# A two-layer hybrid decoder on one Trainium2 core: decay matrices made where they are used, first tiles in another order, a norm factor applied one step later

## The chip, the core and the metric

The kernel runs on one core of a Trainium2 chip. Four engines work side by side, each in the order of its own instruction list: TensorE (PE: matrix products and transposes into PSUM; its weight loads are shown apart as PEld), VectorE (DVE), ScalarE (ACT) and GpSimd (POOL). SyncE (SP) issues nearly all DMAs, also in order: a DMA that has to wait for its data holds up those behind it. The metric is the device time of one execution in microseconds; the time before is the median of three runs.

## The reference

Two layers (DEPTH = 2) of a parallel-branch block on x of 512 x 1024, float32:

```python
h = rmsnorm(x, pre_mix_g)
proj = h @ w_in                     # split: DeltaNet q,k,v,z,beta,decay | SWA q,k,v | gates A,B
y_a = deltanet_branch(...) @ w_up_dn
y_b = swa_sink_branch(...) @ w_up_sw
mix = (sigmoid(gate_a) * y_a + sigmoid(gate_b) * y_b) @ w_o
x = x + rmsnorm(mix, post_mix_g)
ff = square(relu(rmsnorm(x, pre_mlp_g) @ w_ff1)) @ w_ff2
x = x + rmsnorm(ff, post_mlp_g)

# in the DeltaNet branch, per head and chunk, after a causal conv and silu on q, k, v:
g = cumsum(g)
decay = where(i >= j, exp(g_i - g_j), 0)
L = strictly_lower((k * beta) @ k.T * decay);  u, w = solve(I + L, ...)
a_intra = q @ k.T * decay
# scan over the chunks:  v_new = u - w S;  o = q exp(g) S + a_intra v_new;  S = exp(g_last) S + k_dec.T v_new
o = rmsnorm(o, norm_g) * silu(z)
```

DeltaNet has 8 heads of width 128; the sliding-window attention (SWA) has 16 query and 2 key heads of width 64, window 128, with a sink per head.

## The kernel before

All large products are made in three passes on values split in two (`_h` and `_l`): each weight block `wr` (128 x 1024, 512 KB) is loaded by SP, cast to `wh` on ScalarE and its remainder `wl` taken on VectorE (`prefetch`, lines 419 and 420). `weights()` hands out one split block and has the splits made LOOK = 4 blocks ahead; six `wr` buffers stand before them. One unit (`mm_a`, lines 435 to 437) is 24 matmuls of 512 columns into one of two PSUM buffers (`PM`). The kernel is written as one Python program; a planner puts each engine's instructions in order by their place in the program, by when their inputs are ready in its own model of times, and by free buffers. Only where the code opens an `Order` is the written order kept.

A layer runs in stages:

- the first products of a layer (`ps_b`: beta, decay, SWA k and v) for the four token tiles. In layer 0 their order on TensorE, ScalarE, VectorE and SP is written out by hand, with x loaded, normalized (`half`, tile `xs`), transposed (`turn`, `turned`) and the first three weight blocks split (`feed(0)` to `feed(2)`) in between.
- eight SWA query units (`ps_qf`). `q_out` scales and splits each and writes it to the scratch memory `qd`. At the third of them, `decays()` makes the running decay sums, writes them to `gd` (32 x 128), and then, for all eight heads in a loop, the 128 x 512 matrix D: a broadcast load from `gd`, a triangular select on GpSimd, `egl` (the decay of a whole chunk) and four exponentials on ScalarE, and a write to the scratch memory `dd`.
- 16 steps, each with one unit (k of a DeltaNet head, or a gate) and one attention group (`att_group`), whose queries `qT` come from `qd`. A k unit has two halves: `k_unit(h)` up to its `yield` makes the product, conv and silu and stores k; the rest, which is run one step later, loads D from `dd` (line 891), multiplies k by k (`ps_a`) and scales it with D (line 912) into `uu` for the triangular solve. D and `uu` share the four buffers of the tag `T[5]`.
- `solve()`, the up-projection of the attention (`ps_us`), and the DeltaNet heads in turn: `d_chain(h)` is the scan over four chunks (`ps_ks`, `rr` at line 1329, `ps_y` at line 1332, `ps_su`, `St`), beside it `d_dense(h+1)` makes v, q and z of the next head. D is loaded a second time from `dd` there (line 1231).
- the norm of a head's output is a generator, `d_tail(h)`: the mean square goes out to `sd`, comes back as `ff`, gets its power on GpSimd, goes out to `fd`, comes back broadcast as `fb`, and line 1288 multiplies `y1` (`yf`) with it. `d_step` runs the next piece of the heads it names, so each piece lies one call of `d_step` after the one before.
- the up-projection, output projection and the feed-forward part, which the diff does not touch.

Of the kernel before, what the change touches and what calls it, by code (L numbers as in the profile page):

```python
# [10 lines left out]
F32 = mybir.dt.float32  # L11
F32R = mybir.dt.float32r
# [8 lines left out]
P = 128  # L21
# [4 lines left out]
H = 8  # L26
# [117 lines left out]
def hybrid_trunk(ctx, tc, x, positions, pre_mix_g, dn_conv_w, dn_a_log, dn_dt_bias, dn_norm_g,  # L144
# [449 lines left out]
    def turned(ps, t, q):  # L594
        hi, lo = [c4(q[i])[:, :, t * P:(t + 1) * P] for i in range(2)]
        nc.scalar.copy(hi, c4(ps))
        tt(out=lo, in0=c4(ps), in1=hi.bitcast(F32), op=ALU.subtract)
# [52 lines left out]
    for l in range(depth):  # L650
# [4 lines left out]
        if l == 0:  # L655
            order = Order(nc.tensor, nc.scalar, nc.vector, nc.sync)
            order.begin()
            xts = [X4("x0") for t in range(NT)]
            gb, qs, hT = pre_begin(0)
            for i in range(2):  # L660
                dma(xts[0][:, i * 512:(i + 1) * 512], x[0:P, i * 512:(i + 1) * 512])
            wrs = []
            for t in (None, 1, None, 2, None, 3):
                if t is None:
                    wrs.append(load(specs[len(wrs)][0]))
                else:
                    dma(xts[t], x[t * P:(t + 1) * P, :])
            sq = lambda t: (meansq(xts[t][:, :512], "nq0"), meansq(xts[t][:, 512:], "nq1"))
            part = lambda t, a, b: mm_bkv(pb0[t][:, nbs], pre, hT, t, range(a, b))
            half = lambda t, g: norm_half(xts[t], gb, rs[t], g)  # L670
            feed = lambda j: prefetch(j + 1, wrs[j])

            def spin(n):

                for _ in range(n):
                    tr(pb0[2][:, 0:P], ident, ident)

            rs = [root(xts[0])]
            spin(5)
            xs = [half(0, 0), half(0, 1)]  # L680
            ps0 = [turn(x_) for x_ in xs]
            spin(5)
            feed(0)
            turned(ps0[0], 0, qs[0])
            q = [meansq(xts[1][:, :512], "nq0")]
            feed(1)
            q.append(meansq(xts[1][:, 512:], "nq1"))
            rs.append(rstd("nr", *q))
            part(0, 0, 2)
            turned(ps0[1], 0, qs[1])  # L690
            part(0, 2, 4)
            feed(2)
            q = sq(2)
            xs = [half(1, g) for g in range(2)]
            part(0, 4, 5)
            ps1 = [turn(x_) for x_ in xs]
            rs.append(rstd("nr", *q))
            part(0, 5, KT)
            for g in range(2):
                turned(ps1[g], 1, qs[g])  # L700
            q = sq(3)
            xs = [half(2, g) for g in range(2)]
            part(1, 0, 5)
            ps2 = [turn(x_) for x_ in xs]
            rs.append(rstd("nr", *q))
            part(1, 5, KT)
            for g in range(2):
                turned(ps2[g], 2, qs[g])
            xs = [half(3, g) for g in range(2)]
            part(2, 0, 5)  # L710
            ps3 = [turn(x_) for x_ in xs]
            part(2, 5, KT)
            for g in range(2):
                turned(ps3[g], 3, qs[g])
            pb0.append(PS("ps_b"))
            part(3, 0, KT)
            rotary()
            order.end()
            used[0] = 3
        else:  # L720
            hT = hT[2]
            ws = [weights() for _ in BK]
            part = lambda t, a, b: mm_bkv(pb0[t][:, nbs], ws, hT, t, range(a, b))
            part(0, 0, 5)
            part(1, 0, 5)
            part(0, 5, KT)
            part(1, 5, KT)
            qf0 = PZ("ps_qf")
            wq0 = weights()
            mm_a2(qf0, hT, 0, wq0, range(0, 4))  # L730
            norm_turn(xs_next[2], 2, nxt[1])
            mm_a2(qf0, hT, 0, wq0, range(4, KT))
            norm_turn(xs_next[3], 3, nxt[1])
            for a, b in ((0, 5), (5, KT)):
                for t in (2, 3):
                    part(t, a, b)
            mm_a2(qf0, hT, 1, wq0)
            order.end()
# [59 lines left out]
        def decays():  # L798
            ps = PS("ps_g")
            mm(ps[:, 0:32], lhsT=le, rhs=lw, start=True, stop=True)  # L800
            nc.vector.tensor_copy(gc, ps[:, 0:32])
            ts(out=ngc, in0=gc, scalar1=-1.0, scalar2=None, op0=ALU.mult)
            act(out=neg, in_=gc, func=AF.Exp)
            ts(out=neg, in0=neg, scalar1=-1.0, scalar2=None, op0=ALU.mult)
            ps = PS("ps_gt")
            tr(ps[:32, :P], gc, ident)
            gT = sm.tile([32, P], F32, name="gT", bufs=1)
            nc.vector.tensor_copy(gT, ps[:32, :P])
            dma(gd, gT)
            egT = sm.tile([32, P], F32, name="egT", bufs=1)  # L810
            act(out=egT, in_=gT, func=AF.Exp)
            dma(egd, egT)
            for h in range(H):
                d = T[4 + h % 2]("D")
                dma(c4(d), gd[h * NC:(h + 1) * NC, :].partition_broadcast(P))
                nc.gpsimd.affine_select(out=c4(d), in_=c4(d), pattern=[[0, NC], [1, P]],
                                        compare_op=ALU.is_ge, fill=NEG, base=0, channel_multiplier=-1)
                act(out=egl[:, h * NC:(h + 1) * NC], in_=c4(d)[:, :, P - 1], func=AF.Exp)
                for c in range(NC):
                    act(out=d[:, c * P:(c + 1) * P], in_=d[:, c * P:(c + 1) * P], func=AF.Exp,  # L820
                        bias=ngc[:, h * NC + c:h * NC + c + 1])
                dma(dd[h], d)

        rot = [T[2]("rot") for i in range(2)]
        if l == 0:
# [56 lines left out]
        cj, irk = [], []  # L882

        def k_unit(h):
            ps = PM("ps_kp")
            mm_a(ps, hT)
            k_ = conv_silu(ps, 8 + h, T[4], "kk")
            dma(kkd[h], k_)
            yield
            d = T[5]("D")  # L890
            dma(d, dd[h])
            ps = PK("ps_a")
            for c in range(NC):
                sl = slice(c * P, (c + 1) * P)
                mm(ps[:, sl], lhsT=k_[:, sl], rhs=k_[:, sl], start=True, stop=True)
            u_ = T[5]("uu")
            sk_ = sm.tile([P, NC], F32, name="ssk")
            for c in range(NC):
                sl = slice(c * P, (c + 1) * P)
                stt(out=u_[:, sl], in0=ps[:, sl], scalar=1.0, in1=ident, op0=ALU.mult,  # L900
                    op1=ALU.mult, accum_out=sk_[:, c:c + 1])
            ts(out=sk_, in0=sk_, scalar1=EPS, scalar2=None, op0=ALU.add)
            ir = sm.tile([P, NC], F32, name="irk", bufs=H + 1)
            ptt(out=ir, in0=sk_, in1=phalf, op=ALU.pow)
            irk.append(ir)
            cc = sm.tile([P, NC], F32, name="cj", bufs=H + 1)
            nc.vector.reciprocal(cc, sk_)
            tt(out=cc, in0=cc, in1=hc(beta)[:, h, :], op=ALU.mult)
            cj.append(cc)
            for c in range(NC):  # L910
                sl = slice(c * P, (c + 1) * P)
                stt(out=u_[:, sl], in0=ps[:, sl], scalar=cc[:, c:c + 1], in1=d[:, sl],
                    op0=ALU.mult, op1=ALU.mult)
            dma(umat(h), c4(u_))
# [324 lines left out]
        def d_dense(h, after=lambda: None):  # L1239
# [16 lines left out]
            act(out=sz, in_=ps, func=AF.Tanh, scale=0.5)  # L1256
            stt(out=sz, in0=sz, scalar=1.0, in1=ps, op0=ALU.add, op1=ALU.mult)
            after()
            d_step(h - 2)
            qe = T[7]("qe")  # L1260
            ptt(out=qe, in0=qq, in1=egb, op=ALU.mult)

# [7 lines left out]
        def d_tail(h):  # L1270

            w, y1 = dn.pop(("t", h))
            wh, wl = pair(T[5], "w")
            split(w, wh, wl)
            ps = PS("ps_w")
            mm(ps, lhsT=ones_r, rhs=wh, start=True, stop=False)
            mm(ps, lhsT=ones_r, rhs=wl, start=False, stop=True)
            nc.scalar.copy(w[0:1], ps[0:1])
            dma(sd[h:h + 1, :], w[0:1])
            yield  # L1280
            ff = sm.tile([P, NC], F32, name="ff")
            dma(ff, sd[h, :].rearrange("(p j) -> p j", p=P))
            ptt(out=ff, in0=ff, in1=mhalf, op=ALU.pow)
            pdma(fd[h, :].rearrange("(p j) -> p j", p=P), ff)
            yield
            fb = T[6]("fb")
            dma(fb, fd[h, :].partition_broadcast(P))
            tt(out=y1, in0=y1, in1=fb, op=ALU.mult)

        tails = [d_tail(h) for h in range(H)]  # L1290
# [105 lines left out]
        for m in range(NA2, KT):  # L1396
            ga_unit(m)
            d_step(H - 1, H - 2, H - 3)
        yT = []
        for k in range(KT):  # L1400
            p_ = pair(T[4 + k % 4], "yT")
# [360 lines left out]
```

## Time and profile before

| what | value |
|---|---|
| median of three runs | 1819.17 us (1816.89 to 1822.44) |
| the profiled execution's own time | 1820.33 us |
| its span, first to last instruction | 1818.6 us, mean granted clock 0.997 |
| busy: PE, PEld, DVE, ACT, POOL | 1791.7, 1512.3, 1366.6, 997.0, 192.4 us |
| DMA | 296.43 MB, 163 GB/s on average |

How to read the lines: a row of the order of time has start, duration, engine, line of the kernel, operation, written tile, read tiles, and in brackets the idle time before it and what ended it. A list of waits has the waiting engine and tile, what it waited for, and the total, the number and the longest of these waits. A group has its durations in ns (least, median, most), its first and last start and its shape. A busy TensorE is not TensorE at its peak, since matmuls overlap and stretch when the next one comes late.

### The profile page before, as it was taken

To read this page: it belongs to the slowest core of one execution; us is meant where nothing else is said; L and a number is where in the kernel's file an instruction comes from. 1 tells how busy PE (TensorE), PEld (TensorE's weight loads), DVE (VectorE), ACT (ScalarE), POOL (GpSimd) and SP (SyncE) were. 2 spreads that over 40 slices of the span, in tenths; PEclk is the share of its full clock that TensorE was granted. 3 is DMA by queue.
4 is the path that set the end of the run, shared out by engine and by line. 5 is a ranking of instruction groups with operands and counts; after the bars stand their busy time and mean duration, and the time that the engine had idled before them with its cause. 6 is when DMAs were issued, how large, how long until landed. Compare 5 with 4: busy or idle time off the path is not lost.

```text
span 1818.6 us, 28378 instructions
## 1 busy us (share of the span) xinstructions
PE 1791.7 (99%) x10220; PEld 1512.3 (83%) x10220; DVE 1366.6 (75%) x2576; ACT 997.0 (55%) x2039; POOL 192.4 (11%) x346
## 2 busy tenths in 40 slices
PE   9999999999999999999999999999999999999998
PEld 7778878788788888989887887888877888889896
DVE  6489696787665878898574896968875569798973
ACT  6677642444434656566556777324443347566572
POOL 3111102221101000000020121021111010000000
PEclk9999999999999999999999999999999999999999
DMA  6854347665464254554558443485555533555551
GB/s 223 296 162 158 105 146 225 174 168 158 116 197 139 82 162 146 177 181 133 191 186 270 151 156 106 158 233 161 166 142 144 181 116 97 181 160 165 173 177 56
DMA packets 168223, 296.43 MB, mean 163 GB/s; under 512 B 34625, under 2 KB 84097, under 8 KB 168082
## 3 DMA queue, kind: packets, MB, share of 16 engines
q1 hardware_dynamic: 167570, 294.58, 52.1%
q8 instruction: 80, 1.31, 0.3%
q14 instruction: 61, 0.50, 0.1%
q0 software_dynamic: 512, 0.03, 0.0%
HBM read 248.29 MB, written 46.27 MB: 162 GB/s over the span
## 4 chain that ended last, share of the span: by engine, by line
PE 80%; DMA 6%; DVE 4%; ACT 4%; issue 3%; POOL 2%; SPq 1%; DVEq 0%; POOLq 0%; ACTq 0%
PE ps_f L435 2%; PE ps_f L436 2%; PE ps_f L437 2%; PE ps_us L435 2%; PE ps_ud L435 2%; PE ps_b L508 2%; PE ps_us L437 2%; PE ps_b L504 2%; PE ps_ud L436 2%; PE ps_ud L437 2%; PE ps_us L436 2%; PE ps_b L506 2%; PE ps_ga L437 2%; PE ps_ga L436 2%; PE ps_ga L435 2%
## 5 line engine op out<-in xcount | busy, mean ns | idle before, releaser
L419 ACT CAST wh<-wr 128x1024 fp32r<-128x1024 f32 (+2 forms) x366 | 372.8, 1024 | 447.6 <-PE ps_vp L436 61.0
L420 DVE TENSOR_TENSOR wl<-wr,wh 128x1024 fp32r<-128x1024 f32 (+2 forms) x366 | 435.8, 1198 | 183.3 <-ACT wh L419 178.7
L571 POOL TENSOR_TENSOR pr<-pq,pw 128x1 f32<-128x1 f32 x16 | 9.9, 616 | 791.3 <-DVE pq L570 791.3
L435 PE MATMUL ps_f<-g_h,wh 128*128 128x512 f32 x160 | 62.4, 390 | 0.0
L436 PE MATMUL ps_f<-g_l,wh 128*128 128x512 f32 x160 | 62.4, 390 | 0.0
L437 PE MATMUL ps_f<-g_h,wl 128*128 128x512 f32 x160 | 62.2, 389 | 0.0
L436 PE MATMUL ps_qp<-h_l,wh 128*128 128x512 f32 x128 | 54.0, 422 | 0.0
L435 PE MATMUL ps_vp<-h_h,wh 128*128 128x512 f32 x128 | 53.9, 421 | 0.0
L437 PE MATMUL ps_vp<-h_h,wl 128*128 128x512 f32 x128 | 53.6, 419 | 0.0
L435 PE MATMUL ps_kp<-h_h,wh 128*128 128x512 f32 x128 | 52.6, 411 | 0.0
L378 DVE TENSOR_TENSOR wr<-wr 128x512 f32<-128x512 f32 x72 | 47.5, 685 | 6.7 <-DMA wr<-in_weights_dram 5.4
L1059 ACT ACTIVATE M<-M,nm 128x128 f32<-128x128 f32 x128 | 49.8, 391 | 4.9 <-DVE nm L1054 4.8
L435 PE MATMUL ps_qp<-h_h,wh 128*128 128x512 f32 x128 | 51.9, 405 | 0.0
L437 PE MATMUL ps_qp<-h_h,wl 128*128 128x512 f32 x128 | 51.4, 402 | 0.0
L436 PE MATMUL ps_vp<-h_l,wh 128*128 128x512 f32 x128 | 51.3, 401 | 0.0
L435 PE MATMUL ps_gb<-h_h,wh 128*128 128x512 f32 x128 | 51.3, 401 | 0.0
L436 PE MATMUL ps_ga<-h_l,wh 128*128 128x512 f32 x128 | 51.0, 398 | 0.0
L437 PE MATMUL ps_kp<-h_h,wl 128*128 128x512 f32 x128 | 51.0, 398 | 0.0
L436 PE MATMUL ps_kp<-h_l,wh 128*128 128x512 f32 x128 | 50.9, 398 | 0.0
L435 PE MATMUL ps_ga<-h_h,wh 128*128 128x512 f32 x128 | 50.5, 395 | 0.0
L437 PE MATMUL ps_ga<-h_h,wl 128*128 128x512 f32 x128 | 50.5, 394 | 0.0
L436 PE MATMUL ps_gb<-h_l,wh 128*128 128x512 f32 x128 | 50.3, 393 | 0.0
(448 smaller groups left out, 5944.5 us busy)
## 6 DMA issues: line engine op xcount, KB each, us to landing
wr<-in_weights_dram SPq DMA_DIRECT2D x336, 512.0 KB
D<-dd SPq DMA_DIRECT2D x32, 256.0 KB
qT<-qd SPq DMA_DIRECT2D x32, 256.0 KB
xd<-xo SPq DMA_DIRECT2D x12, 512.0 KB
xt<-xd SPq DMA_DIRECT2D x24, 256.0 KB
qd<-qf_h SPq DMA_DIRECT2D x16, 256.0 KB
qd<-qf_l SPq DMA_DIRECT2D x16, 256.0 KB
D<-gd SPq DMA_DIRECT2D x16, 256.0 KB
```

Of the source, the lines that this page charges most:

```text
L378: tt(out=o_, in0=i0, in1=i1, op=ALU.add)
L419: nc.scalar.copy(wh[:, :w], wr[:, :w])
L420: sub(out=wl[:, :w], in0=wr[:, :w], in1=wh[:, :w].bitcast(F32), op=ALU.subtract)
L435: mm(ps, lhsT=wh[:, k, :], rhs=hi, start=k == 0, stop=False)
L436: mm(ps, lhsT=wh[:, k, :], rhs=lo, start=False, stop=False)
L437: mm(ps, lhsT=wl[:, k, :], rhs=hi, start=False, stop=k == KT - 1)
L504: mm(pss[t], lhsT=hi[:, tsl], rhs=wh[:, r, :], start=k == 0 and not onto, stop=False, skip_group_check=onto)
L506: mm(pss[t], lhsT=hi[:, tsl], rhs=wl[:, r, :], start=False, stop=False, skip_group_check=onto)
L508: mm(pss[t], lhsT=lo[:, tsl], rhs=wh[:, r, :], start=False, stop=k == KT - 1, skip_group_check=onto)
L571: ptt(out=r, in0=q1, in1=mhalf[:, 0:1], op=ALU.pow)
L1059: act(out=M[:, j * P:(j + 1) * P], in_=M[:, j * P:(j + 1) * P], func=AF.Exp, bias=nm[:, j:j + 1], accum_out=den[:, j:j + 1])
```

## The change

Three edits. (1) The loop over the heads leaves `decays()`. `k_unit(h)` starts with the load of its D from `gd` (`decay_load`), makes D behind its own conv and silu (`decay_of`: select, `egl`, four exponentials, the write to `dd`), and its second half uses that tile; the load of D from `dd` in the k unit is gone. `dd` is still written, for the second use in the DeltaNet stage. (2) In layer 0 the first two weight blocks are loaded before the second tile of x; the second block's cast stands ahead of the first tile's, its remainder behind the first products, and the third block's split behind the second tile's scaling. (3) `d_tail` has a step of its own between the load of `fb` and the multiplication; `d_dense` steps one head more, and a last `d_step` follows the loop.

```diff
-            for t in (None, 1, None, 2, None, 3):
+            for t in (None, None, 1, None, 2, 3):
...
+            def first_cast():
+                wh, wl = [wp.tile([P, 1024], F32R, name=n_, bufs=LOOK) for n_ in ("wh", "wl")]
+                w = width(specs[1][1])
+                held = wh[:, :w], wl[:, :w], wrs[1][:, :w]
+                one.append((held, (blocks(wh, specs[1][1]), blocks(wl, specs[1][1]))))
+                return held[0], held[2]
+
+            def first_rest():
+                (wh, wl, wr), both = one.pop()
+                tt(out=wl, in0=wr, in1=wh.bitcast(F32), op=ALU.subtract)
+                pre.append(both)
+
+            one = []
...
             feed(0)
+            nc.scalar.copy(*first_cast())
             turned(ps0[0], 0, qs[0])
+            part(0, 0, 2)
+            first_rest()
             q = [meansq(xts[1][:, :512], "nq0")]
-            feed(1)
             q.append(meansq(xts[1][:, 512:], "nq1"))
+            turned(ps0[1], 0, qs[1])
             rs.append(rstd("nr", *q))
-            part(0, 0, 2)
-            turned(ps0[1], 0, qs[1])
             part(0, 2, 4)
+            part(0, 4, 5)
+            xs = [half(1, g) for g in range(2)]
             feed(2)
             q = sq(2)
-            xs = [half(1, g) for g in range(2)]
-            part(0, 4, 5)
             ps1 = [turn(x_) for x_ in xs]
...
-            for h in range(H):
-                d = T[4 + h % 2]("D")
-                dma(c4(d), gd[h * NC:(h + 1) * NC, :].partition_broadcast(P))
-                nc.gpsimd.affine_select(out=c4(d), in_=c4(d), pattern=[[0, NC], [1, P]],
-                                        compare_op=ALU.is_ge, fill=NEG, base=0, channel_multiplier=-1)
-                act(out=egl[:, h * NC:(h + 1) * NC], in_=c4(d)[:, :, P - 1], func=AF.Exp)
-                for c in range(NC):
-                    act(out=d[:, c * P:(c + 1) * P], in_=d[:, c * P:(c + 1) * P], func=AF.Exp,
-                        bias=ngc[:, h * NC + c:h * NC + c + 1])
-                dma(dd[h], d)
+
+        def decay_load(h):
+            d = T[5]("D")
+            dma(c4(d), gd[h * NC:(h + 1) * NC, :].partition_broadcast(P))
+            return d
+
+        def decay_of(h, d):
+            nc.gpsimd.affine_select(out=c4(d), in_=c4(d), pattern=[[0, NC], [1, P]],
+                                    compare_op=ALU.is_ge, fill=NEG, base=0, channel_multiplier=-1)
+            act(out=egl[:, h * NC:(h + 1) * NC], in_=c4(d)[:, :, P - 1], func=AF.Exp)
+            for c in range(NC):
+                act(out=d[:, c * P:(c + 1) * P], in_=d[:, c * P:(c + 1) * P], func=AF.Exp,
+                    bias=ngc[:, h * NC + c:h * NC + c + 1])
+            dma(dd[h], d)
...
         def k_unit(h):
+            d = decay_load(h)
             ps = PM("ps_kp")
             mm_a(ps, hT)
             k_ = conv_silu(ps, 8 + h, T[4], "kk")
             dma(kkd[h], k_)
+            decay_of(h, d)
             yield
-            d = T[5]("D")
-            dma(d, dd[h])
             ps = PK("ps_a")
...
-            d_step(h - 2)
+            d_step(h - 2, h - 3)
...
             dma(fb, fd[h, :].partition_broadcast(P))
+            yield
             tt(out=y1, in0=y1, in1=fb, op=ALU.mult)
...
             d_step(H - 1, H - 2, H - 3)
+        d_step(H - 1)
```

## The prediction

> **What bounds the kernel now.** I read the page first (who is busy), then TensorE's waits, then busy time by stage, then the order of time around the places that the change touches.
>
> ```profile
> span 1818.6 us, 28378 instructions
> ...
> PE 1791.7 (99%) x10220; PEld 1512.3 (83%) x10220; DVE 1366.6 (75%) x2576; ACT 997.0 (55%) x2039; POOL 192.4 (11%) x346
> ...
> PE ps_s L1041 <- DMA qT<-qd: 3.4, 2, 1.9
> PE ps_y L1332 <- DVE rr L1329: 2.9, 5, 1.8
> PE ps_qf L435 <- DVE qf_l L838: 2.8, 2, 1.4
> ...
> PE ps_n L591 <- DVE xs L580: 1.3, 1, 1.3
> ```
>
> TensorE is busy 1791.7 of 1818.6 us: only 26.9 us in which it does nothing. No edit here removes a matmul, so the change can win only idle TensorE time, or time in which its clock is low. The four waits above are those the edits aim at, 10.4 us together (columns: total, times, longest). That alone says: a gain of some tenths of a per cent, not more.
>
> ```profile
> 50.00:90.00 40.00, 36.99 (x170) 30.25 (x170) 15.38 (x28) 23.52 (x68) 5.10 (x8) 1.00 0.91 301
> 100.00:180.00 80.00, 79.39 (x419) 65.63 (x418) 72.46 (x224) 62.30 (x188) 14.87 (x18) 1.00 0.49 156
> 1000.00:1080.00 80.00, 79.26 (x417) 65.25 (x416) 72.45 (x226) 62.03 (x188) 14.84 (x18) 1.00 0.49 156
> 987.00:994.00 7.00, 7.00 (x23) 5.85 (x23) 6.32 (x16) 5.45 (x21) 0.00 (x0) 0.53 0.80 259
> ```
>
> Columns: stretch, PE, PEld, DVE, ACT, POOL busy, granted clock, DMA share, GB/s. In layer 0 the decay matrices are made in 50 to 70 us, inside the SWA q units; that stretch leaves 3.0 us of TensorE idle, with the DMA engines 91% busy. The k units follow (100 to 180 us; 1000 to 1080 us in layer 1): TensorE loses 0.6 us there, and ScalarE has 17.7 us free of 80. The last row is layer 1's stretch just behind its own decays: TensorE is "busy" throughout, but at a mean clock of 0.53.
>
> **The decay matrices, the main edit.** What a head costs:
>
> ```profile
> L820 ACT ACTIVATE D<-D,ngc x64: 385/388/404, 55.3 to 966.3; 128x128 f32<-128x128 f32 x64
> L815 SPq DMA_DIRECT2D D<-gd x16: 394/430/448, 50.2 to 957.2; - x16
> L816 POOL TENSOR_SCALAR_AFFINE_SELECT D<-D x16: 637/638/644, 54.3 to 961.9; 128x512 f32<-128x512 f32 x16
> L818 ACT ACTIVATE egl<-D x16: 191/194/211, 55.0 to 964.4; 128x4 f32<-128x4 f32 x16
> L822 SPq DMA_DIRECT2D dd<-D x16: 319/320/320, 56.6 to 966.7; - x16
> L891 SPq DMA_DIRECT2D D<-dd x16: 424/497/535, 73.1 to 1076.2; - x16
> ...
> 50.00:70.00 20.00, 9.89 (x32) 1.00 0.88 299
> ```
>
> The last row is line 820 alone: 32 exponentials fill 9.89 us in a layer (they overlap a little), 1.24 us a head; with the small one about 1.35 us of ScalarE, 0.64 us of POOL, a 256 KB load from gd and a 256 KB write to dd. Removed: the sixteen reloads of line 891. No wait for them stands in any answer, so their own worth is nothing. All the rest moves into the k unit. T[5] has four buffers, two of which the first two uu take, so I expect two heads still to be made early and six a layer beside the k units. It leaves behind:
>
> ```profile
> 62.02 3.61 ACT L820 ACTIVATE D<-D,ngc 128x128 f32<-128x128 f32 x12
> ...
> 67.76 0.57 ACT L837 ACTIVATE qf_h<-ps_qf 128x512 fp32r<-128x512 f32 x1
> ...
> 69.11 0.50 PE L435 MATMUL ps_qf<-h_h,wh 128*128 128x512 f32 x1 [1.43 <-DVE qf_l L838]
> ...
> 967.93 0.50 PE L435 MATMUL ps_qf<-h_h,wh 128*128 128x512 f32 x1 [1.32 <-DVE qf_l L838]
> ```
>
> Twelve exponentials in a row hold up qf_h, so the two PSUM buffers of the q units come free late, and TensorE idles 1.43 and 1.32 us. With two heads instead of eight in the burst this wait should go: **-2.75 us** (bounds 0 and -2.75; late next is the q unit's own copy, 0.57 us, which a unit of 24 matmuls hides).
>
> ```profile
> 40.47 2.11 SPq L316 DMA_DIRECT2D wr<-in_weights_dram  x2
> ...
> 69.46 0.45 SPq L316 DMA_DIRECT2D wr<-in_weights_dram  x1
> ...
> 77.60 0.32 SPq L841 DMA_DIRECT2D qd<-qf_l  x1
> 77.97 0.96 SPq L316 DMA_DIRECT2D wr<-in_weights_dram  x2
> 81.50 2.03 SPq L1018 DMA_DIRECT2D qT<-qd  x4
> ...
> 86.78 0.30 PE L1041 MATMUL ps_s<-kT_h,qT 128*128 128x128 f32 x1 [1.57 <-DMA qT<-qd]
> ...
> 985.92 0.30 PE L1041 MATMUL ps_s<-kT_h,qT 128*128 128x128 f32 x1 [1.86 <-DMA qT<-qd]
> ```
>
> During the burst SP issues no weight load from 42 to 69 us; the late weights then share the DMA engines with the last q write and the first qT loads, and attention's first scores wait 1.57 and 1.86 us. Taken out of that stretch are six loads and six to eight writes of 256 KB, 3.1 to 3.7 MB: at the 301 GB/s of the first row 10 to 12 us of DMA time. But the chain last qf_l, qd, qT starts as much earlier as TensorE does, so only the shorter landings count. I take half: **-1.7 us** (0 to -3.4).
>
> The low clock: 7 us at 0.53 lose 7 x 0.47 = 3.3 us. It begins within 1 us of the 1.86 us wait; the 1.57 us wait of layer 0 was followed by none (1.00 in the first row). If the wait shrinks below 1.57 us the drop should not come: **-3.3 us** (0 to -3.3). [...]
>
> What it adds: six heads x 1.35 = 8.1 us of ScalarE to a stage with 17.7 us free, so 88% busy, and 0.64 us of POOL per head in front of attention's two selects. Both engines work in order: an exponential whose select or load is late holds the casts and softmax behind it. The loads depend only on gd, written long before, and buffers come free early, so most should fill idle time. Bounds: nothing, and all eight heads' work on TensorE's path, 8 x 1.35 = 10.8 us a layer, 21.6 us in all. TensorE lost only 0.6 us in 80 with ScalarE at 78%, so I sit near the lower end: 1 us a layer, **+2.0 us**. On SP, the dd write now waits for ScalarE with weight loads behind it; weights are split four units ahead, which covers it: 0, or what that last upper bound holds already.
>
> **The norm factor.** Line 1288 now runs one step after its load:
>
> ```profile
> L1288 DVE TENSOR_TENSOR yf<-yf,fb x16: 682/693/693, 358.8 to 1406.9; 128x512 f32<-128x512 f32 x16
> its engine sat idle before it (us, times) until:
>   DMA fb<-fd: 26.8, 13
> ...
> 358.77 0.69 DVE L1288 TENSOR_TENSOR yf<-yf,fb 128x512 f32<-128x512 f32 x1 [2.26 <-DMA fb<-fd]
> 359.38 0.35 DVE L1329 SCALAR_TENSOR_TENSOR rr<-ps_ks,neg,vs 128x128 f32<-128x128 f32 x1
> ...
> 359.78 0.49 PE L1332 MATMUL ps_y<-rr,Pt 128*128 128x128 f32 x2 [1.78 <-DVE rr L1329]
> ```
>
> VectorE stands 26.8 us at it, but only where the chain's rr is behind it does TensorE feel it: the 2.9 us of the second list. I take **-2.5 us** (0 to -2.9). The fb tile lives half a step longer; T[6] hands its buffer to egb of the next dense step, needed a whole head later: 0. The last head's product has no later step and runs where it did: 0.
>
> **The first tiles.**
>
> ```profile
> 12.39 1.01 DVE L420 TENSOR_TENSOR wl<-wr,wh 128x816 fp32r<-128x816 f32 x1
> 13.31 1.40 DVE L580 SCALAR_TENSOR_TENSOR xs<-x,nr,ps_row 128x512 f32<-128x512 f32 x2
> 14.11 1.38 PE L591 MATMUL ps_n<-ident,xs 128*128 128x128 f32 x8 [1.26 <-DVE xs L580]
> 15.24 0.37 PE L456 MATMUL ps_b<-wh,h_h 128*128 128x272 f32 x1
> ```
>
> The second tile's xs go ahead of the third weight split, so the transposes start up to 1.0 us sooner; but that split (1.01 us) then ends 1.40 us later, about 14.9, and the products that need it started at 15.24. **-0.3 us**, between -1.3 (the whole gap) and +1.4 (x of the second tile lands behind one more weight block of 408 KB, 1.4 us at 301 GB/s).
>
> **The sum.** -2.75 - 1.7 - 3.3 + 2.0 - 2.5 - 0.3 = -8.55 us. The profiled execution took 1820.33 us (span 1818.6), 1.2 us above the median of the runs, 1819.17; so 1811.8 us on its own scale, and 1810.6 on the median's: I say 1811. About 0.3%, 5.5 us, is what a measurement here can tell from no change.
>
> **The rivals.**
> *The transfer is the bound anyway.* The qT wait stays near 1.86 us, and the low clock behind it: -8.55 + 1.7 + 3.3 = -3.6 us, 1815.6 on the median's scale, no change that can be told. For it: qd and qT hang on each other and start only after the last q unit. Against: 3 MB less traffic ahead of them. 0.18.
> *The low clock stays alone.* The wait shrinks, but the 7 us at 0.53 come all the same, because something other than this wait brings them: -8.55 + 3.3 = -5.25 us, 1814, just inside what counts as the same. For it: one drop in one execution is all the trace has, and only 0.3 us part the wait that had a drop behind it from the one that had none. Against: the drop begins right behind the wait. 0.10. [...]
> *ScalarE becomes the k stage's bound (slower).* The exponentials sit in its queue ahead of casts and softmax, with a select and a load before them, and all of their time reaches TensorE: 21.6 instead of 2.0 us, so -8.55 + 19.6 = +11, 1830. It decides for slower by over 0.3% once the k stages lose 16 us together, 1.0 us a head. For it: VectorE is 91% busy there, so a late ScalarE meets no slack. Against: 17.7 us of free ScalarE time, four units of split weights. 0.16.
> *All of it goes and the k stages hide their part.* -2.75 - 3.4 - 3.3 - 2.9 - 1.3 = -13.7 us, 1805.5. 0.18.
> *Forecast,* 1811: 0.38.
>
> **How the numbers follow.** Faster 0.38 + 0.18 = 0.56, same 0.18 + 0.10 = 0.28, slower 0.16. The range reaches from under the best case (1805.5 less 1.5, about half the spread between the lowest and the highest run shown, 1816.89 and 1822.44) to the slower rival at three fifths of its price, 1811 + 0.6 x 19.6 = 1823: 1804 to 1823. The forecast's own range is 1807 to 1814.5.
>
> **What would show it.** In the changed profile line 820 runs from about 55 us on into the k stage, two heads before it; ps_qf no longer waits for qf_l; ps_s waits under 1.57 us for qT and the granted clock stays 1.00 behind 985 us; fb is gone from VectorE's waits and ps_y waits under 1 us. The k stages show ScalarE near 88% and TensorE still over 79 of 80 us. Wrong would be: new waits of ps_o, ps_a or ps_kp in the k stages, POOL selects of pc held up behind D's select, or the clock at about 0.5 in layer 1 as before.

## The result, and the profile after

The change makes the kernel slower: 1824.53 us (median of 9 runs, 1821.68 to 1829.92) against 1818.87 us (9 runs, 1815.5 to 1822.54), a ratio of 1.0033, 95% interval [1.0023, 1.0042]. The forecast was 1811. The profiled execution took 1826.57 us, 2.0 us above its median.

The page, and TensorE's list of waits (what waited, for what, total, times, longest):

```profile
span 1824.8 us, 28361 instructions
...
PE 1790.6 (98%) x10220; PEld 1509.3 (83%) x10220; DVE 1370.3 (75%) x2576; ACT 998.1 (55%) x2039; POOL 196.6 (11%) x346
```

```profile
PE ps_o L1106 <- ACT pf_h L545: 6.2, 8, 1.9
PE ps_o L1106 <- POOL pc L1100: 4.5, 6, 1.4
PE ps_y L1352 <- DVE rr L1349: 3.9, 4, 2.5
...
PE ps_s L1060 <- DMA qT<-qd: 1.9, 2, 1.0
```

`ps_qf <- qf_l` (2.8 us) is gone and `qT` fell from 3.4 to 1.9 us, as foreseen. Attention's last product `ps_o` now waits 10.7 us for `pf_h` (a cast on ScalarE) and `pc` (a select on GpSimd), where it waited 2.1 us before:

```profile
PE ps_o L1087 <- POOL pc L1081: 1.1, 2, 0.6
PE ps_o L1087 <- ACT pf_h L545: 1.0, 2, 0.5
```

The wait for `rr`, which the norm edit should have ended, is still there (3.9 us, 2.9 before).

Busy time by stage, same columns as before:

```profile
50.00:90.00 40.00, 39.06 (x181) 32.27 (x180) 16.51 (x33) 18.05 (x46) 1.52 (x2) 1.00 0.76 236
100.00:180.00 80.00, 76.06 (x400) 61.50 (x398) 69.00 (x211) 67.25 (x213) 17.38 (x22) 1.00 0.51 158
1000.00:1080.00 80.00, 74.71 (x395) 60.68 (x393) 67.83 (x201) 65.19 (x205) 18.21 (x22) 1.00 0.51 154
987.00:994.00 7.00, 7.00 (x37) 5.88 (x36) 5.63 (x13) 6.20 (x23) 0.00 (x0) 1.00 0.50 164
```

In 50 to 90 us TensorE's idle time falls from 3.0 to 0.9 us. In the two 80 us stretches of the k stages it rises from 0.6 and 0.7 us to 3.9 and 5.3 us. ScalarE, with 67.3 and 65.2 of 80 us, is not the bound there. The clock behind 987 us is whole in this execution.

Where the new waits come from, in the order of time (layer 0, then layer 1):

```profile
130.86 0.46 SPq L933 DMA_DIRECT2D ud<-uu  x1
131.37 0.50 SPq L831 DMA_DIRECT2D D<-gd  x1
...
134.49 0.32 SPq L831 DMA_DIRECT2D D<-gd  x1
...
136.66 0.63 POOL L835 TENSOR_SCALAR_AFFINE_SELECT D<-D 128x512 f32<-128x512 f32 x1 [0.93 <-DMA D<-gd]
137.25 0.65 POOL L1100 TENSOR_SCALAR_AFFINE_SELECT pc<-pf_l 128x512 fp32r<-128x512 f32 x1
137.33 0.21 ACT L837 ACTIVATE egl<-D 128x4 f32<-128x4 f32 x1 [2.24 <-POOL D L835]
...
137.95 0.51 PE L1106 MATMUL ps_o<-pc,vp 128*128 128x512 f32 x1 [1.40 <-POOL pc L1100]
...
1068.56 0.21 ACT L837 ACTIVATE egl<-D 128x4 f32<-128x4 f32 x1 [2.74 <-POOL D L835]
...
1072.92 1.27 ACT L839 ACTIVATE D<-D,ngc 128x128 f32<-128x128 f32 x4
...
1075.13 0.58 ACT L545 CAST pf_h<-ps_pt 128x512 fp32r<-128x512 f32 x1
...
1075.77 0.50 PE L1106 MATMUL ps_o<-pf_h,vp 128*128 128x512 f32 x1 [1.86 <-ACT pf_h L545]
```

The load of D needs a buffer of `T[5]`: in this trace SP waits for the write of an `uu` (`ud<-uu`) ahead of four of these loads, 5.2 us in all. In layer 0 SP issues it right behind the write of an `uu` (130.86, then 131.37). The select at 136.66 us waits for a load, 5.3 us after the earlier of the two shown was issued. Two things stand behind that select in order: on GpSimd `pc`, whose lateness costs TensorE 1.40 us, and on ScalarE `egl`, which holds that engine for 2.24 us. In layer 1 ScalarE stands 2.74 us at `egl`; 4 us later four exponentials come ahead of `pf_h`, and `ps_o` waits 1.86 us. Who waited for D in the whole execution (total, times):

```profile
who waited for it (us, times):
  POOL D L835: 25.6, 10
  ACT egl L837: 19.1, 10
```

Three of these ten selects stand in the q units, where GpSimd has little else to do, and hold 21.5 of the 25.6 us; in the kernel before, eight selects wait 37.3 us there. What is new stands in the k stages: seven selects wait 4.1 us for their load, and six `egl` 11.2 us for their select (none did there before).

### The profile page after: what moved, and what is told of

It is laid out like the page before. It is cut to its first block, busy times and chain, and to the rows that moved or that the text cites. A ratio compares the mean times of both kernels' runs of the same rounds, so it can differ in the third digit from the quotient of the medians.

```text
span 1824.8 us, 28361 instructions
## 1 busy us (share of the span) xinstructions
PE 1790.6 (98%) x10220; PEld 1509.3 (83%) x10220; DVE 1370.3 (75%) x2576; ACT 998.1 (55%) x2039; POOL 196.6 (11%) x346
## 4 chain that ended last, share of the span: by engine, by line
PE 79%; DMA 6%; ACT 6%; DVE 4%; issue 2%; POOL 1%; SPq 1%; DVEq 0%; POOLq 0%; ACTq 0%
PE ps_f L436 2%; PE ps_f L435 2%; PE ps_f L437 2%; PE ps_us L435 2%; PE ps_ud L435 2%; PE ps_b L504 2%; PE ps_us L437 2%; PE ps_b L508 2%; PE ps_b L506 2%; PE ps_ud L437 2%; PE ps_ud L436 2%; PE ps_us L436 2%; PE ps_ga L437 1%; PE ps_ga L435 1%; PE ps_ga L436 1%
## 5 line engine op out<-in xcount | busy, mean ns | idle before, releaser
L435 PE MATMUL ps_us<-oT_h,wh 128*128 128x512 f32 x128 | 50.0, 390 | 0.4 <-DVE qq L893 0.3
L437 PE MATMUL ps_gb<-h_h,wl 128*128 128x512 f32 x128 | 50.2, 392 | 0.0
```

Of the source, the lines that this page charges most:

```text
L435: mm(ps, lhsT=wh[:, k, :], rhs=hi, start=k == 0, stop=False)
L437: mm(ps, lhsT=wl[:, k, :], rhs=hi, start=False, stop=k == KT - 1)
```

## The experiments

Each ratio is to the kernel before, run beside it on the same chip (1817.6 to 1817.9 us), with its 95% interval. "Idle" in the tables is an 80 us stretch, 100 to 180 or 1000 to 1080 us, less TensorE's busy time in it: 0.6 and 0.7 us before, 3.9 and 5.3 us after. A trace is one execution: that of only_decay took 1827.19 us (median 1823.55), that of decay_early 1815.46 (median 1819.25), so those two differ in their traces by more than in their medians.

### The three edits alone

**only_decay**: the decay edit of the diff, without the other two.

> The kernel before with the decay edit alone (no change to the first tiles and the norm factor). Theory: the loss comes from the k stages. In the changed kernel the stretches 80 to 260 us and 980 to 1160 us lost 3.9 and 3.5 us against before, and the q units won 1.2 and 1.7 us, so about +4.5 us: 1823.4 against 1818.9, with ps_o waiting for pf_h and pc in the k stages. Rival: the decay edit is near neutral and the loss comes from the other two edits: under 1820.5.

1.0036 [1.0023, 1.0048]. It carries the whole loss. TensorE's waits, and who waited for D:

```profile
PE ps_o L1091 <- POOL pc L1085: 4.8, 5, 1.7
PE ps_o L1091 <- ACT pf_h L545: 4.8, 8, 1.3
```

```profile
  POOL D L820: 24.4, 9
  ACT egl L822: 18.5, 10
```

**only_first**: the first-tiles edit alone.

> The kernel before with the edit of the first tiles alone. By the two traces TensorE lost 0.6 us more in the first 40 us of the changed kernel than before: +0.6 us, 1819.5, not to be told from no change. Rival: it carries the loss, over +3 us.

0.9995 [0.9986, 1.0004]: no difference that shows.

**only_norm**, the norm edit alone, and **norm_kept**, the same with the product's place on VectorE fixed:

```diff
-            tt(out=y1, in0=y1, in1=fb, op=ALU.mult)
+            tc.keep_in_program_order(tt(out=y1, in0=y1, in1=fb, op=ALU.mult))
```

> The kernel before with the extra step of the norm factor alone. Theory: the planner puts the product where its own model believes fb landed, so the extra step in the program does not move it on VectorE; fb is still waited for 26 us and the time is the same, 1818 to 1820.5. Rival (the prediction's term): -2.5 us, 1816.4, with fb's waits gone.

> As only_norm, but the product is pinned behind everything written before it on VectorE, behind the dense step's sz, so that it really runs a step later. Theory: VectorE's waits for fb inside the chain go (the two at the very end of each layer stay, 9 us of VectorE each), ps_y waits under 1 us for rr, and the time falls by about 2.5 us, to 1816.4. Rival: the waits of VectorE go and the time stays, because other work takes up the place: 1818 to 1820.

0.9999 [0.9988, 1.001] and 1.0002 [0.9993, 1.001]. In the changed kernel VectorE's idle time at the product, and the product's place in time:

```profile
  DMA fb<-fd: 26.4, 11
```

```profile
362.61 0.69 DVE L1308 TENSOR_TENSOR yf<-yf,fb 128x512 f32<-128x512 f32 x1 [2.98 <-DMA fb<-fd]
363.22 0.34 DVE L1349 SCALAR_TENSOR_TENSOR rr<-ps_ks,neg,vs 128x128 f32<-128x128 f32 x1
```

The extra step in the program did not move the product on VectorE: it still stands ahead of `rr`. Fixing its place in norm_kept does: VectorE waits for `fb` 4 times instead of 11, and TensorE's wait for `rr` (2.9 us before) leaves the list. But two waits come in that the list of before does not have, and the time doesn't move:

```profile
PE ps_su L1338 <- DVE yy L1335: 1.8, 4, 0.7
...
PE ps_ud L436 <- DVE yT_l L546: 1.2, 2, 0.6
```

### What in the k units costs

**k_busy**, the kernel before with four exponentials more in each k unit that nobody uses, and **k_busy2** with two of them:

```diff
             dma(kkd[h], k_)
+            jk = sm.tile([P, P], F32, name="jk2", bufs=1)
+            for c in range(NC):
+                act(out=jk, in_=k_[:, c * P:(c + 1) * P], func=AF.Exp)
             yield
```

> The kernel before, with decay matrices by way of scratch memory as before, plus four exponentials of 128x128 in each k unit, read from its own k and written to a scratch tile that nothing reads: the same ScalarE time as the change adds to the k stages, without a load or a select in front. Theory late load: work alone is absorbed by ScalarE's free time, at most +1.5 us, 1819 to 1820.5. Rival sheer work: +4 us or more for the 16 x 1.2 us, 1823 or above.

> As k_busy with two exponentials of 128x128 in each k unit in place of four: half the dose, written to a tile that nothing reads. Theory work: the loss goes with the work, +2.5 us, about 1820. Rival: it goes with the planner's other order as such and not with the amount, so about the +5 us of k_busy, or none.

1.0028 [1.0017, 1.0039] and 1.0019 [1.0004, 1.0034]; idle 2.3 and 2.0 us, and 1.3 and 1.3 us. ScalarE's work in this stage is not free, though it had 17.7 of 80 us to spare. By that alone the exponentials looked like the cause; the next run speaks against it.

**decay_noexp**, only_decay without the exponentials:

```diff
-            dma(c4(d), gd[h * NC:(h + 1) * NC, :].partition_broadcast(P))
+            dma(c4(d), egd[h * NC:(h + 1) * NC, :].partition_broadcast(P))
...
-            for c in range(NC):
-                act(out=d[:, c * P:(c + 1) * P], in_=d[:, c * P:(c + 1) * P], func=AF.Exp,
-                    bias=ngc[:, h * NC + c:h * NC + c + 1])
```

> As only_decay with the four exponentials of each head left out: load, select, egl and the write to dd stay in the k unit. It leaves out part of the computation (D holds exp(g) of the column, loaded from egd in place of gd, not the decay). Theory work: k_busy lost 0.28% by the exponentials alone, so without them the k stages lose little and the shorter q units are left: 2 to 4 us under the kernel before, 1814 to 1816. Rival late load: select and egl still stand in front of other work waiting for the load; half or more of the 6 us of only_decay stays, 1821 or above.

1.0048 [1.0031, 1.0065]: with the 9.9 us of the 32 exponentials taken off ScalarE in each layer it is no faster than only_decay. Part of that is the clock: the granted clock of its six runs is 0.9967 on average, 0.9983 in the kernel before, an estimated 2.9 us (0.0016 of 1818). Without that it would be at about the loss of only_decay, so the exponentials are not most of what the edit loses by. `ps_o` now waits on GpSimd:

```profile
PE ps_o L1088 <- POOL pc L1082: 9.0, 8, 2.0
```

**decay_early**, only_decay with D in buffers of another tag, two heads to a tile, so that the loads needn't wait for `uu`; **decay_kept**, only_decay with the select's and `egl`'s places in the order fixed as written:

```diff
-            d = T[5]("D")
+            if h % 2 == 0:
+                dx.append(X4("Dx"))
+            d = dx[-1][:, h % 2 * 512:(h % 2 + 1) * 512]
```

> As only_decay, but D lives in halves of the 1024-wide tiles of the tag x4 and no longer shares the four buffers of T[5] with uu, so its load need not wait for the buffer of an earlier uu. Theory late load: POOL's select and ScalarE's egl stand in front of other work and wait for a load that is issued only when a buffer comes free; with earlier loads egl waits for the select under half of the 11 us that it waited in the two k stages, and the time falls by 2 to 4 us from only_decay, to 1820. Rival sheer work: the 1.35 us of ScalarE a head is the cost, and the time stays within 1 us of only_decay.

> As only_decay, but the select and egl are pinned behind everything written before them on their engines, so the planner cannot put them ahead of older work of POOL and ScalarE on the belief that the load has landed. Theory late load: the waits of egl for the select shrink and the time falls by 2 to 4 us from only_decay, to 1820. Rival sheer work: within 1 us of only_decay, 1822 to 1824.5. Third way: the pinned select itself holds up attention's selects behind it, and the time is higher than only_decay.

1.0012 [1.0, 1.0024] and 1.0029 [1.002, 1.0038]. Other buffers take back two thirds of the loss (idle 2.6 and 2.7 us). Their loads are not early, eight selects still wait 13.9 us for them in the k stages, but `egl` waits for none of these selects (10.3 us in only_decay's k stages). The other order takes back hardly any (idle 3.3 and 2.5 us), against the theory in its expectation: `egl`'s waits for the select are gone altogether, and `ps_o`'s for `pf_h` and `pc` fall from 9.6 to 5.6 us, but the time falls by 0.07% only, less than the intervals. So ScalarE's stand at `egl` doesn't carry the loss alone.

**early_merged**: as decay_early, and the running sum subtracted on GpSimd, so that one exponential of 512 columns a head stands in place of four and `egl`.

```diff
+            ptt(out=c4(d), in0=c4(d), op=ALU.add,
+                in1=ngc[:, h * NC:(h + 1) * NC].unsqueeze(2).broadcast_to([P, NC, P]))
...
+            act(out=d, in_=d, func=AF.Exp)
```

> As decay_early (D in its own buffers, made in the k units), with the subtraction on POOL and one exponential of 128x512 a head. Theory work: the k stages lose half as much as with decay_early, so 2 to 4 us under it, 1814 to 1817. Rival: POOL's extra 1.3 us a head holds up attention's selects (pc) and ps_o waits for them: 1819 or above.

1.0052 [1.0033, 1.007]. ScalarE has less to do, but GpSimd more, with `pc` behind it: `ps_o` waits 6.8 us for `pc`, and ScalarE 16.2 us for GpSimd. Here more in GpSimd's queue ahead of `pc` costs more than less on ScalarE saves (decay_early: 1.0012).

### The load by itself

**decay_noload**: all the work of only_decay, at its place, but every select reads one row that was loaded long before.

```diff
+        g0 = sm.tile([P, 512], F32, name="g0", bufs=1)
...
-            dma(c4(d), gd[h * NC:(h + 1) * NC, :].partition_broadcast(P))
...
-            nc.gpsimd.affine_select(out=c4(d), in_=c4(d), pattern=[[0, NC], [1, P]],
+            nc.gpsimd.affine_select(out=c4(d), in_=c4(g0), pattern=[[0, NC], [1, P]],
```

> The kernel before with the decay edit alone, but without its eight loads a layer: the row of head 0 is loaded once a layer into a tile of its own (512 elements a partition), behind the write of gd, and each head's select in its k unit reads that tile and writes its own D; egl, the four exponentials and the write to dd stay, with the bias of head 0. Left out: the decays of the other seven heads. All the work on GpSimd and ScalarE is in the k units, and nothing there can come late from a DMA. Theory (the late load, behind which GpSimd and then ScalarE stand still, carries most of the loss): a ratio at 1.0005 to 1.002 (1818.7 to 1821.5 against 1817.8), ps_o waits for pc under 2 us in all, egl waits for the select under 4 us; what is left is the price of the moved work, as k_busy (+0.28%, half of it +0.19%) less what the q units win. Rival (the select and the exponentials in these two in-order queues are the price whether or not the load is in time): 1.003 or more, the TensorE's lost time in 80 to 260 us at about 14 us as with the whole decay edit (10.5 before).

0.9995 [0.9984, 1.0005], 0.41% under only_decay and a little under the theory's range. Idle 2.0 and 2.1 us. `egl` waits 5.8 us (4) for the select, somewhat more than expected, `pc` costs TensorE 0.6 us. But the traffic is gone with the lateness.

**decay_ahead** keeps the traffic: the whole edit with each head's own row, loaded two heads ahead into a tile with two buffers of its own.

```diff
+        def decay_row():
+            h = len(gs)
+            if h < H:
+                gs.append(sm.tile([P, 512], F32, name="gx", bufs=2))
+                dma(c4(gs[h]), gd[h * NC:(h + 1) * NC, :].partition_broadcast(P))
...
-            nc.gpsimd.affine_select(out=c4(d), in_=c4(d), pattern=[[0, NC], [1, P]],
+            nc.gpsimd.affine_select(out=c4(d), in_=c4(gs[h]), pattern=[[0, NC], [1, P]],
...
             decay_of(h, d)
+            decay_row()
```

> The decay edit alone, whole and with every head's own row, but with its load in time: the row of a head from gd goes into a tile of its own with two buffers, loaded two heads ahead (the first two behind the write of gd, the next one behind each head's select), and the select reads it and writes D. The traffic is that of the edit; what differs from decay_noload is only the loads themselves, seven more of 256 KB a layer. Theory (lateness of the load, not its traffic): as decay_noload, 0.999 to 1.001 (1816 to 1819.6), egl waits for the select under 4 us, ps_o waits for pc under 2 us. Rival (decay_noload won because the loads' traffic was gone): 1.0025 or more, as only_decay (1.0036), with the weights or qT late. Second rival (two buffers don't make it early enough: the row of h + 2 is asked for when the select of h is done, and SP issues it behind others): in between, 1.001 to 1.0025, with selects that still wait for their load.

0.9986 [0.9975, 0.9997]: the rival with the traffic falls, and the edit, so mended, is slightly faster than the kernel before. Its stretches, what the select and `egl` waited for, and TensorE's waits:

```profile
100.00:180.00 80.00, 77.96 (x408) 63.62 (x408) 70.22 (x216) 69.20 (x217) 17.93 (x23) 1.00 0.52 162
1000.00:1080.00 80.00, 77.78 (x406) 63.23 (x406) 69.90 (x219) 69.67 (x223) 17.93 (x23) 1.00 0.51 161
```

```profile
  DMA gx<-gd: 13.5, 2
...
  POOL D L826: 4.4, 4
```

```profile
PE ps_o L1100 <- ACT pf_h L545: 3.3, 5, 1.1
...
PE ps_o L1100 <- POOL pc L1094: 0.8, 3, 0.3
```

Both of these selects stand in the q units; in the k stages none waits for its load (six in only_decay), and `egl` waits 0.35 us there for the select (10.3 in only_decay). `pc` costs 0.8 in place of 4.8 us. GpSimd itself stands idle 12.3 us ahead of six selects in the k stages, for `uu`, its write and attention's `nm`; so GpSimd's waiting as such is not what costs. A load asked for two heads ahead turns 1.0036 into 0.9986 here. Two things stay joined with it: with a tile of its own for the row, D also takes its `T[5]` buffer only when its select runs, and the planner puts select, `egl` and exponentials in another order. Which of these, the earlier issue, the shorter hold or the order, gives how much, was not tried.

**q_pinned_busy**: q_pinned (below) with k_busy's exponentials, to see whether gain and price add.

> q_pinned (0.9972) with the four extra 128x128 exponentials in each k unit of k_busy (1.0028), which no one uses. If what the edit wins in the q units and what its exponentials cost in the k units simply add, this has both and is at 0.9995 to 1.0 (1817 to 1818), the ratio of decay_noload (0.9995), which has both too. Rival (in k_busy the extra work cost so much because the k stages began late behind the burst, and with the burst gone it finds room): 0.9975 or under, as q_pinned, and then the loss of k_busy isn't the price that the edit pays.

1.0013 [1.0002, 1.0024], above both expectations. The exponentials of k_busy cost 0.41% here, but those of decay_ahead, beside the same gain, 0.14%. k_busy's read `kk`, which has just been made, and ScalarE waits for it (2.0 us, twice, in 100 to 180 us of this run); the edit's read a row that came early. k_busy was too dear a stand-in, which the run shows; that the wait for `kk` is all of the difference, it does not show, and 0.14% is known to about 0.16% to either side only.

### The gain in the q units, without the k units

**spread**: decays stay in the q units, one or two heads behind each unit's q_out, loads and selects too.

```diff
+                for h in ((0, 1), (2,), (3,), (4,), (5,), (6, 7))[u - 2]:
+                    decay(h)
```

> The kernel before with the loop of decays() taken apart: D is still made in the q units and goes by way of scratch memory, but the heads are written behind the q units one after the other (two behind the third, one each behind the next four, two behind the last), so that ScalarE never has twelve exponentials in a row ahead of qf_h. Theory: the waits of ps_qf (1.4 and 1.3 us) go and the k stages lose nothing, -2.5 to -7 us, 1812 to 1816.5 with the low clock of layer 1 gone. Rival: the exponentials of the last heads now fall into the first attention group and ps_s, ps_a or ps_o wait instead: 1818 or above.

1.0035 [1.0022, 1.0047]. The same fault in another place: a load issued late (68.89), a select that waits for it, `egl` that waits for the select, and the last `qf_h` behind it:

```profile
68.89 1.97 SPq L816 DMA_DIRECT2D D<-gd  x1
...
75.23 0.64 POOL L817 TENSOR_SCALAR_AFFINE_SELECT D<-D 128x512 f32<-128x512 f32 x1 [6.75 <-DMA D<-gd]
75.90 0.21 ACT L819 ACTIVATE egl<-D 128x4 f32<-128x4 f32 x1 [4.43 <-POOL D L817]
78.26 0.59 ACT L838 ACTIVATE qf_h<-ps_qf 128x512 fp32r<-128x512 f32 x1
...
89.35 0.45 PE L1044 MATMUL ps_s<-kT_h,qT 128*128 128x128 f32 x1 [4.01 <-DMA qT<-qd]
```

By the granted clock much of this loss is half clock: 0.9958 on average in its five runs, 0.9986 in the kernel before, an estimated 5 of the 6.4 us.

**q_merged**: the kernel before with early_merged's subtraction on GpSimd and one exponential a head, in the q units.

> The kernel before, D made in the q units by way of scratch memory, but the subtraction of g_j is done on POOL (1.3 us a head, 40 us with 5 us of POOL busy) so that ScalarE makes one exponential of 128x512 a head (about 0.6 us) in place of four and a small one (1.35 us); egl comes from one more small product with ones. ScalarE's burst falls from 10.8 to about 5 us a layer and the k stages stay as they were. Theory: ps_qf's waits (2.75 us) go, the qT wait gets shorter: -2.5 to -6 us, 1812 to 1815.5. Rival: D comes later by POOL's work and the burst moves onto the qT loads, as with spread: 1819 or above.

1.0071 [1.0054, 1.0088]: `ps_qf` waits 11.7 us (4, longest 4.4) for `qf_l`, since ScalarE stands 25.0 us at the exponentials for GpSimd, with `qf_h` behind them (clock 0.9952 on average, an estimated 5.6 us of it).

**q_last**: loads and selects as before, `egl` and the exponentials written behind the last q unit. **q_pinned**: the same loads and selects, and the exponentials of two heads behind each q_out of the fourth to seventh unit, their order on ScalarE fixed:

```diff
+                if 3 <= u <= 6:
+                    decay_exp(2 * u - 6)
+                    decay_exp(2 * u - 5)
```

**q_pinned_first** adds the first-tiles edit.

> The kernel before with the loads and selects where they were, and egl, the exponentials and the writes to dd written in the program behind the last q unit, not pinned: the planner places them, and by its own order puts twelve or thirteen in a row between two qf_h again. Theory that the planner's place on ScalarE, not the place in the program, decides: no change, 0.999 to 1.001, with the wait of ps_qf for qf_l still at 2 to 3 us. Theory that being written later is enough: as the pinned one, under 0.999.

> The kernel before, with nothing moved into the k units: the loads and selects of all eight heads stay at the third q unit, but egl and the exponentials are taken out of the one burst: those of two heads stand, in the written order of ScalarE, behind each of the fourth to seventh q unit's q_out. If the gain of the edit lies in the q units (ps_qf waiting for qf_l, qT late behind the burst) and its loss in the k units, this keeps the gain and pays no loss: 0.9965 to 0.999 (1811.5 to 1816), ps_qf no longer waits for qf_l, qT waits under 1.0 us, the k stages lose what they lost before (10.5 and 13.3 us in 80 to 260 and 980 to 1160). Rival (the q units' gain is only moved on: the k stages start earlier and meet the same weights and loads): 0.9995 to 1.001. Second rival (two heads behind each q_out, 2.7 us, still hold qf_h up, or wait for a late select as in the run with spread decays): over 1.001, with ps_qf or qT waits of over 2 us.

> The same with the change's first-tiles edit beside it: if the two add, 0.9995 of the one without (the first tiles alone gave 0.9995 [0.9986, 1.0004]), so 0.996 to 0.9985; no difference to the one without is what the earlier run makes likelier.

0.9987 [0.9979, 0.9996], 0.9972 [0.996, 0.9983] and 0.997 [0.9958, 0.9982]. In q_last the planner still put twelve exponentials in a row, but the wait for `qf_l` went, and the time falls just inside its second theory. The count in a row was the wrong one: in the kernel before, 24 exponentials stand between two `qf_h` (58.06 and 67.76 us), the twelve of the prediction and these:

```profile
58.06 0.58 ACT L837 ACTIVATE qf_h<-ps_qf 128x512 fp32r<-128x512 f32 x1
58.54 2.44 ACT L820 ACTIVATE D<-D,ngc 128x128 f32<-128x128 f32 x8
...
66.58 1.27 ACT L820 ACTIVATE D<-D,ngc 128x128 f32<-128x128 f32 x4
```

In q_last at most 13 stand between two, in q_pinned eight. q_pinned beats the kernel before by 5.1 us (1812.85 against 1817.92) and the changed one by more; the first tiles add nothing that shows. q_pinned by stage, and its first scores:

```profile
50.00:90.00 40.00, 39.92 (x185) 33.01 (x184) 18.49 (x35) 25.97 (x75) 5.91 (x8) 1.00 0.97 322
100.00:180.00 80.00, 79.37 (x423) 66.07 (x423) 72.48 (x224) 63.39 (x191) 14.50 (x18) 1.00 0.49 153
...
1000.00:1080.00 80.00, 79.17 (x415) 65.31 (x415) 71.72 (x225) 64.39 (x198) 16.69 (x20) 1.00 0.48 151
```

```profile
84.56 0.30 PE L1052 MATMUL ps_s<-kT_h,qT 128*128 128x128 f32 x1
```

TensorE is idle 0.1 us in 50 to 90 us, the k stages are as before, and the first scores wait for no `qT`, with the DMA engines 97% busy.

### The sizes together

| step | from, to | change |
|---|---|---|
| gain in the q units | before, q_pinned | -0.28%, -5.1 us |
| the work in the k units, its row in time | q_pinned, decay_ahead | +0.14%, +2.5 us |
| the load late, with the longer hold of `T[5]` | decay_ahead, only_decay | +0.50%, +9.1 us |
| whole decay edit | before, only_decay | +0.36%, +6.5 us |

(Per cent of 1817.8 us. The sum closes by construction; each step is a difference of two measured ratios whose intervals are 0.11 to 0.13% to either side, so a step between two runs is known to about 0.17%: +0.14% is not told from nothing, +0.50% is. decay_ahead also differs from q_pinned in the q units: its first scores wait 1.9 us for `qT`, those of q_pinned not at all.) With decay_noload in decay_ahead's place the two middle steps are +0.23% and +0.41%.

## Why the prediction was wrong

- **`ps_qf`, -2.75 us: right.** The wait is gone in the changed kernel. Not twelve but 24 exponentials stood ahead of that `qf_h`, as shown at q_last.
- **`qT`, -1.7 us: right in size, wrong in reason.** It fell by 1.5 us (3.4 to 1.9). But I put it down to 3 MB less traffic; in q_pinned all of that traffic is there and the wait is gone. What goes with it is how many exponentials stand together on ScalarE: 24 before, 13 in q_last (2.4 us), eight in q_pinned (no wait).
- **The low clock, -3.3 us: not a term that a median could give.** Behind 987 us it was absent in the profiled execution of the changed kernel, but half clock comes and goes between executions (0.996 to 1.000 on average over a run, in nine runs of the changed kernel), and the average stayed: 0.9982 in these nine, 0.9983 to 0.9986 in those of the kernel before, so the term gave nothing that shows. The rule behind it, that a wait under 1.57 us has no drop behind it, was my estimate from two waits, and no run shows it: one of 1.68 us had a drop behind it in only_first, one of 2.11 us had none in k_busy (last section).
- **The k stages, +2.0 us: here the sum failed.** The work itself came to 2.5 us (decay_ahead against q_pinned; 4.2 by decay_noload), each to about 3 us, so nothing here speaks against its size. What failed is the sentence "The loads depend only on gd, written long before, and buffers come free early, so most should fill idle time". The four buffers of `T[5]` are shared with `uu`; the load is issued only when one of them is free (131.37 us, right behind an `uu`'s write), and lands after the place where its select stands in GpSimd's order. That, with the hold of the buffer and the order that go with it, cost 9.1 us more; how it splits stays open. I had named the danger ("an exponential whose select or load is late holds the casts and softmax behind it"), and could have read from the trace when each `ud<-uu` frees a buffer, but gave it no price of its own.
- **The norm factor, -2.5 us: wrong twice.** The product stayed ahead of `rr`, because a later place in the program is not a later place on VectorE; and where norm_kept moved it, the wait of 2.9 us went, the two others shown there (3.0 us) came, and the time stayed: 1.0002. That the one turned into the others is not shown.
- **The first tiles, -0.3 us:** 0.9995 [0.9986, 1.0004] allows it.

The rival "ScalarE becomes the k stage's bound" had the sign and the place (`pf_h`, and selects in front of `pc`), not the cause: ScalarE is at 84 and 81% in the changed kernel, where I expected 88, and without the exponentials the loss is no smaller. Its chance of 0.16 rested on the work's length; the lateness of one load with two in-order queues behind it deserved a rival of its own. The lower end of the range has a slip: half the spread of the runs named (1816.89 to 1822.44) is 2.8 us, not 1.5.

## What to carry to other kernels

When work moves beside other work, ask for each operand that arrives by DMA what frees the buffer that the load goes into: the issue time is that, not the time when the data exist (here 131.37 us, right behind the write of an `uu` at 130.86). An instruction that waits for it holds all behind it on its engine, and the engines that wait for those (here ScalarE 2.24 us at `egl`, TensorE 1.40 us behind `pc`); a tile of its own for the operand, asked for two uses ahead, turned +0.36% into -0.14%. And a burst on one engine can be broken up where it stands, with loads and selects left early (0.9972), before it is moved to another stage.

## What the runs showed of the hardware

TensorE's granted clock fell to 0.50 for some us behind some short waits, and not behind others. In the kernel before it stood at 0.50 for 6.83 us (986.79 to 993.62), from 0.9 us behind the end of the 1.86 us wait for `qT`. In spread it sets in 0.6 us before the end of the 4.01 us wait shown above, and in only_first 1.4 us behind the end of one of 1.68 us for `qT` (ended at 983.83 us); in k_busy a wait of 2.11 us ended at 87.52 us with the clock whole. Stretches of these three, in that order:

```profile
88.70:95.50 6.80, 6.15 (x23) 5.60 (x24) 4.00 (x10) 3.19 (x11) 0.00 (x0) 0.50 0.90 279
```

```profile
981.78:985.19 3.41, 1.73 (x12) 1.34 (x11) 0.66 (x2) 0.00 (x0) 0.00 (x0) 1.00 0.85 251
985.19:988.60 3.41, 3.41 (x14) 3.03 (x13) 3.01 (x8) 3.02 (x11) 0.00 (x0) 0.50 0.80 266
```

```profile
83.69:87.10 3.41, 1.71 (x8) 1.09 (x6) 0.92 (x4) 0.52 (x2) 0.00 (x0) 1.00 1.05 318
87.10:90.51 3.41, 3.00 (x21) 2.83 (x22) 2.15 (x6) 1.36 (x4) 0.00 (x0) 1.00 0.75 250
```

So the length of a wait doesn't tell by itself whether half clock follows: 1.68 us had it behind it, 2.11 us had not. Nor does TensorE's busy time in a stretch of 3.41 us: 1.73 us just ahead of only_first's drop, 1.71 us in the first stretch of k_busy, with the clock whole in the next. What decides is not shown.
